# A generalized delta-rule scan in chunks: the grams of two heads as one padded 128-column product, or as two 64-row products with a bank each

## The chip, the core and the metric

The kernel runs on one core of a Trainium2 chip. The metric is the device time of one launch in microseconds: 2266.26 is the median of two runs of the kernel before, 2266.1 and 2266.43. Its engines are TensorE (PE; its weight loads are shown apart, as PEld), VectorE (DVE), ScalarE (ACT), GpSimd (POOL) and SyncE (SP, which issues the transfers).

## The reference, cut to what matters

The program is a backbone of two layers, an attention layer and a layer of RWKV-7 time mixing, each followed by an MLP. The change lies in the scan of the second layer. It runs over 256 context tokens and then 512 latent tokens, in both directions, for 16 heads of 64 features:

```
def step(s, inp):                       # s: one 64x64 state per head
    r_t, w_t, k_t, v_t, a_t, b_t = inp
    sa = jnp.einsum('bhvk,bhk->bhv', s, a_t)
    s = s * w_t[:, :, None, :] + sa[..., None] * b_t[:, :, None, :] + v_t[..., None] * k_t[:, :, None, :]
    return s, jnp.einsum('bhvk,bhk->bhv', s, r_t)
...
s_fwd, yc_fwd = wkv_scan(rc, decc[0], kc, vc, nac, bc, zero, False)      # context first
_, y_fwd = wkv_scan(r, dec[0], k, v, na, b, s_fwd, False)                # latents start from its last state
```

The kernel does not take one token at a time. It cuts the tokens into chunks of 64 and needs, for every chunk, head and direction, the masked products ("grams") of the chunk's scaled b and k vectors with its scaled a and r vectors.

## The kernel before, in words

**Groups.** The function `rwkv_scan` goes through six groups, `its[0]` to `its[5]`: a context group of four feature tiles (8 heads, 4 chunks), then two latent groups of two feature tiles each (4 heads, 8 chunks), and all this a second time for the other half of the features. A feature tile holds 128 features, that is two heads: head e=0 on partitions 0 to 63, head e=1 on 64 to 127. Every group has the scaled vectors `AR` (a and r, 64 columns each) and `BK` (b and k, 64 columns each), laid out by direction d and block (feature tile, chunk), and the grams `GM`. There are two sets of these three, used in turn: group n+2 overwrites what group n has read.

**What a group goes through.** `prep` loads the features and makes AR and BK (L1213 to L1217, after two exponentials on ScalarE, L1200 and L1201), and calls `grams` with x=0 for every feature tile and direction. `lanes` solves the triangular systems of the chunks on VectorE: a transpose (L1285) and then 30 steps of a product and a sum (L1295, L1298). `merge` brings the result back with two transposes (L1303, L1306), small matmuls (L1313, L1321) and copies into GM. `late` calls `grams` with x=1 (latent groups only, the columns of r), scales BK to the chunk's end (`to_end`, L1259) and, in `turn`, transposes BK (L1337). `chain` is the recurrence over chunks: `x_ps` (L1382, L1385), a copy `xsb`, `u_ps` (L1397), a copy into `z`, `s_ps` (L1412), and the new state `sn` on VectorE (L1423); latent groups also make the outputs `y_ps` (L1433, L1437), copied to `yt` (L1439). A chain step needs the state of the step before. `readout` normalizes and gates the outputs.

**What sets the order.** The code writes `merge` of group n+1, `prep`, `lanes` and `late` of group n+2 and so on one after the other, with `late` and the readout handed out piece by piece between the steps of the chain; a scheduler then decides, with its own estimate of each instruction, in which order every engine gets them. Each engine carries out its queue strictly in that order. The first context group's `prep` lies among the projection of v, before the scan's own memory is opened; there the grams use the PSUM tags "a" and "o". Inside the scan, all grams, the transposes of BK and the small matmuls of `merge` share a tag "g" of two banks (`gtile`).

**Grams before.** `grams(it, fl, d, x)` takes one feature tile and direction, four chunks at a time. BK of a block (128 partitions, 128 columns) is the stationary operand. AR of the two heads must not be mixed, so ScalarE copies it into one of two tiles `pad` of twice the width, head 0 into the upper half of the partitions of the left columns, head 1 into the lower half of the right columns; the other quarters were set to zero at the start (L1134). One matmul per chunk with all 128 rows then gives both heads side by side, 128 columns, and four chunks fill a bank. VectorE multiplies the bank with the mask `gmask` and writes it to GM. float32 matmuls appear in the trace as two records each.

Of the kernel before, what the change touches and what calls it, by code (L numbers as in the profile page):

```python
# [9 lines left out]
F32 = mybir.dt.float32  # L10
F32R = mybir.dt.float32r
AF = mybir.ActivationFunctionType
ALU = mybir.AluOpType
# [7 lines left out]
P = 128  # L21
# [60 lines left out]
def rconst_layout():  # L82
    names = [("gmask", 256), ("sel", 8 * 32), ("bsel", 8 * 128), ("gsel", 4 * 32), ("gbsel", 4 * 128),
             ("cen", 128), ("blk", 128)]
    off, out = 0, {}
    for n, w in names:
        out[n] = (off, w)
        off += w
    return out, off
# [56 lines left out]
LM = ()  # L146
# [24 lines left out]
class K:  # L171
# [909 lines left out]
    def rwkv_scan(self, xsave, osave):  # L1081


        nc, a, tc, ctx = self.nc, self.a, self.tc, self.ctx
# [4 lines left out]
        sa = st.enter_context(tc.tile_pool(reuse_waits=RW.get("scan_a", "pool"), name="scan_a", bufs=1))  # L1089
        rl, _ = rconst_layout()  # L1090

        def rload(name, pool, dt=F32):
            o, w = rl[name]
            t = pool.tile([P, w], dt, name=f"s_{name}")
            if dt == F32:
                nc.sync.dma_start(t, a["rconsts"][:, o:o + w])
            else:
                raw = sp.tile([P, w], F32, tag="f4", bufs=NF4, name=f"sr_{name}")
                nc.sync.dma_start(raw, a["rconsts"][:, o:o + w])
                nc.vector.tensor_copy(t, raw)  # L1100
            return t

        gmask = rload("gmask", sa).rearrange("p (d x) -> p d x", d=2)
# [10 lines left out]
        def gtile(name):  # L1114

            if pp is not None:
                return pp.tile([P, 512], F32, tag="g", bufs=2, name=name)
            gbank[0] ^= 1
            return self.ps.tile([P, 512], F32, tag="ao"[gbank[0]], name=name)
# [7 lines left out]
        lane = pa.tile([P, 32 * 32], F32, tag="lane", name="lane")  # L1127
        Lt = lane.rearrange("p (t s) -> p t s", t=32)
        MT = sa.tile([P, 32, 32], F32, tag="mt", name="mt")
        padn = [0]  # L1130
        pads = [sa.tile([P, 2, 256], F32, name=f"pad{i}") for i in range(2)]
        for t in pads:
            for e in range(2):
                nc.gpsimd.memset(t[64 - 64 * e:128 - 64 * e, e], 0.0)  # L1134

        class It:
            pass
# [15 lines left out]
        def prep(it):  # L1153
# [33 lines left out]
            def part(fl, d):  # L1187
# [28 lines left out]
                if it.lat:  # L1216
                    nc.vector.tensor_tensor(ar[:, :, 64:128], src[fl, "r"], ep[:, :, inc], ALU.mult)  # L1217
                nc.gpsimd.tensor_scalar(it.PC[:, :, fl, d], ends, 1.0, 0.0, ALU.mult, ALU.add)
                grams(it, fl, d, 0)

            return [lambda fl=fl, d=d: part(fl, d) for fl in range(it.nf) for d in range(2)]

        def grams(it, fl, d, x):


            nh, nch = it.nh, it.nch
            xs = slice(64 * x, 64 * x + 64)
            for c0 in range(0, nch, 4):
                pad = pads[padn[0] % len(pads)]
                padn[0] += 1  # L1230
                pv = pad.rearrange("p e (k x) -> p e k x", k=4)
                b = fl * nch + c0
                for e in range(2):
                    r = slice(64 * e, 64 * e + 64)
                    nc.scalar.activation(pv[r, e], it.AR[r, d, b:b + 4, xs], AF.Copy)  # L1235
                g = gtile("g_ps")
                for k in range(4):
                    nc.tensor.matmul(g[:, P * k:P * k + P], it.BK[:, d, b + k], pv[:, :, k], start=True, stop=True)  # L1238
                out = it.GM[:, d].rearrange("p (c h) x -> p c h x", h=nh)[:, c0:c0 + 4, 2 * fl:2 * fl + 2, xs]
                if x and (d, c0 // 4) in LM:  # L1240
                    nc.scalar.activation(out, g.rearrange("p (k e x) -> p k e x", k=4, e=2), AF.Copy)
                    nc.gpsimd.tensor_tensor(out, out, gmask[:, d, xs].unsqueeze(1).unsqueeze(1).to_broadcast([P, 4, 2, 64]), ALU.mult)
                    continue
                nc.vector.tensor_tensor(out, g.rearrange("p (k e x) -> p k e x", k=4, e=2),  # L1244
                                        gmask[:, d, xs].unsqueeze(1).unsqueeze(1).to_broadcast([P, 4, 2, 64]), ALU.mult)

        def late(it):

            def part(fl, d):
                if it.lat:  # L1250
                    grams(it, fl, d, 1)
                to_end(it, fl, d)

            return [lambda fl=fl, d=d: part(fl, d) for fl in range(it.nf) for d in range(2)] + [lambda: turn(it)]
# [523 lines left out]
```

## Time and profile before

| | us |
|---|---|
| median of the runs | 2266.26 |
| the profiled execution, whole | 2270.0 |
| its span from first to last instruction | 2268.2 |
| TensorE, busy | 2049.9 |
| VectorE, busy | 1320.1 |
| ScalarE, busy | 857.2 |
| ScalarE, the 160 copies into `pad` (L1235), mean of one | 0.41 |
| TensorE, the 640 records of the grams (L1238), busy | 98.1 |
| VectorE, the 80 masks (L1244), median of one | 0.684 |

All views of the profile come from the one profiled execution, and the times in them count from the start of its span. The grams are in it from 1300.3 to 1738.4 us. A row of the timeline gives start, length, engine, line, operation, output and inputs, shapes, and how many instructions are merged in it; brackets give the idle time ahead and who ended it. Lines are those of the kernel before.

### The profile page before, as it was taken

The page shows a single profiled execution, that of the slowest core. Times are in us where ns is not written, and L with a number is a line of the kernel's source. Part 1 is how long each engine was busy: PE and PEld are TensorE (multiplying, and loading weights), DVE is VectorE, ACT ScalarE, POOL GpSimd, SP SyncE. Part 2 cuts the span into 40 slices and gives each one's busy share as a digit, 9 for nine tenths or more (in the row PEclk, how much of TensorE's full clock was granted, in tenths as well). Part 3 has the DMA queues.
Part 4 walks back from the last instruction along what each step waited for, and adds up shares of the span by engine and source line. Part 5 has one row for each costly group of instructions (what it writes and reads, how often), then busy time and mean ns, then how long its engine had stood idle before and what let it go on. Part 6 is the DMA issues. An engine that isn't in the chain of part 4 may idle for free. (4 is left out here: it accounts for less than half of the span.)

```text
span 2268.2 us, 40460 instructions
## 1 busy us (share of the span) xinstructions
PE 2049.9 (90%) x16208; PEld 1668.3 (74%) x16208; DVE 1320.1 (58%) x2737; ACT 857.2 (38%) x1702; POOL 263.7 (12%) x362
## 2 busy tenths in 40 slices
PE   5989999979999999997979798698869887999999
PEld 4876756868888888885856687586658655787887
DVE  4465565464334343349787665888898657444443
ACT  4344454232111111116454445567647433222121
POOL 0122232010000000001010101000000101101110
PEclk9999999989999999997999898789889898999999
DMA  8344461122122121116146434113311312323322
GB/s 288 102 135 135 138 212 58 56 79 65 61 61 66 56 70 61 53 37 236 63 162 244 135 129 155 35 51 90 95 48 58 128 56 79 103 93 95 96 88 80
DMA packets 115885, 229.67 MB, mean 101 GB/s; under 512 B 12912, under 2 KB 31088, under 8 KB 115312
## 3 DMA queue, kind: packets, MB, share of 16 engines
q1 hardware_dynamic: 115696, 227.08, 31.1%
q8 instruction: 128, 2.10, 0.4%
q14 instruction: 61, 0.50, 0.1%
HBM read 191.80 MB, written 32.60 MB: 99 GB/s over the span
## 5 line engine op out<-in xcount | busy, mean ns | idle before, releaser
L337 DVE TENSOR_TENSOR wlo<-wraw,whi 128x1024 fp32r<-128x1024 f32 (+1 forms) x121 | 134.5, 1120 | 322.6 <-ACT whi L334 169.2
L364 PE MATMUL w_ps<-mhl,whi 128*128 128x512 f32 (+1 forms) x768 | 235.7, 361 | 7.3 <-DVE mhl L317 7.3
L362 PE MATMUL w_ps<-mhh,whi 128*128 128x512 f32 (+1 forms) x768 | 235.1, 361 | 7.1 <-POOL whi L336 3.4
L366 PE MATMUL w_ps<-mhh,wlo 128*128 128x512 f32 (+1 forms) x768 | 235.4, 361 | 5.0 <-DVE wlo L337 5.0
L364 PE MATMUL w_ps<-hid,w2h 128*128 128x512 f32 (+1 forms) x768 | 234.0, 359 | 0.0
L362 PE MATMUL w_ps<-hid,w2h 128*128 128x512 f32 (+1 forms) x768 | 231.4, 355 | 1.6 <-ACT mrelu L689 1.4
L366 PE MATMUL w_ps<-hid,w2l 128*128 128x512 f32 (+1 forms) x768 | 231.1, 355 | 0.0
L334 ACT ACTIVATE w2h<-w2raw 128x512 fp32r<-128x512 f32 x64 | 40.4, 631 | 330.0 <-PE w_ps L364 299.1
L660 DVE SCALAR_TENSOR_TENSOR X<-w_ps,ada,X 128x256 f32<-128x256 f32 (+1 forms) x128 | 73.1, 612 | 137.5 <-PE w_ps L366 137.5
L364 PEld LDWEIGHTS w_ps<-mhl,whi 128*128 128x128 f32 x768 | 127.7, 190 | 33.0 <-DVE mhl L317 9.8
L362 PEld LDWEIGHTS w_ps<-mhh,whi 128*128 128x128 f32 x768 | 127.8, 190 | 31.7 <-POOL whi L336 4.1
L366 PEld LDWEIGHTS w_ps<-mhh,wlo 128*128 128x128 f32 x768 | 127.8, 190 | 31.0 <-DVE wlo L337 8.0
L336 POOL TENSOR_SCALAR whi<-wraw 128x1024 fp32r<-128x1024 f32 (+1 forms) x60 | 69.2, 1154 | 673.2 <-PE w_ps L364 252.6
L366 PEld LDWEIGHTS w_ps<-hid,w2l 128*128 128x128 f32 x768 | 127.4, 189 | 23.3
L362 PEld LDWEIGHTS w_ps<-hid,w2h 128*128 128x128 f32 x768 | 125.5, 188 | 24.8 <-ACT mrelu L689 2.3
L334 ACT ACTIVATE whi<-wraw 128x1024 fp32r<-128x1024 f32 (+1 forms) x61 | 59.1, 968 | 222.7 <-PE w_ps L364 100.8
L364 PEld LDWEIGHTS w_ps<-hid,w2h 128*128 128x128 f32 x768 | 126.6, 188 | 20.7
L689 ACT ACTIVATE mrelu<-w_ps 128x768 f32<-128x768 f32 (+1 forms) x64 | 44.7, 699 | 189.6 <-PE w_ps L366 189.6
L1238 PE MATMUL g_ps<-pad,bk 128*128 128x128 f32 x640 | 98.1, 306 | 6.1 <-DVE gm L1244 2.1
L1238 PEld LDWEIGHTS g_ps<-pad,bk 128*128 128x128 f32 x640 | 86.0, 212 | 15.9 <-ACT pad L1235 7.5
L564 DVE CUSTOM_DVE_ANT_0 sm<-sc_ps,consts,vecs 128x256 f32<-128x256 f32 (+2 forms) x96 | 71.6, 760 | 40.7 <-PE pt_ps L585 21.9
L337 DVE TENSOR_TENSOR w2l<-w2raw,w2h 128x512 fp32r<-128x512 f32 x128 | 89.1, 697 | 4.8 <-ACT w2h L334 4.6
(381 smaller groups left out, 4486.1 us busy)
## 6 DMA issues: line engine op xcount, KB each, us to landing
ada_w<-ada_w SPq DMA_DIRECT2D x160, 256.0 KB, 3.5
wraw<-w SPq DMA_DIRECT2D x64, 512.0 KB, 3.2
w2raw<-w SPq DMA_DIRECT2D x128, 256.0 KB, 2.6
kt<-ada_w SPq DMA_DIRECT2D x32, 256.0 KB, 5.1
feat<-cs SPq DMA_DIRECT2D x16, 390.0 KB, 2.3
cs<-feat SPq DMA_DIRECT2D x24, 260.0 KB, 3.1
wraw<-wq SPq DMA_DIRECT2D x8, 512.0 KB, 3.8
wraw<-wo SPq DMA_DIRECT2D x8, 512.0 KB, 3.2
```

Of the source, the lines that this page charges most:

```text
L334: nc.scalar.activation(hi, raw, AF.Copy)
L336: nc.gpsimd.tensor_scalar(hi, raw, 1.0, 0.0, ALU.mult, ALU.add)
L337: nc.vector.tensor_tensor(lo, raw, hi.bitcast(F32), ALU.subtract)
L362: nc.tensor.matmul(o, wh, cut(xh, sl), start=start, stop=False)
L364: nc.tensor.matmul(o, wh, cut(xl, sl), start=False, stop=False)
L366: nc.tensor.matmul(o, wl, cut(xh, sl), start=False, stop=stop)
L564: nc.vector.tensor_tensor_reduce(sm[:, :nk], ps[:, :nk], self.c["band"][:, b0:b0 + nk], rs[:, h:h + 1], self.v["sink"][:, hd:hd + 1], ALU. ...
L660: self.nc.vector.scalar_tensor_tensor(self.X[:, m, sl], ps[:, sl], self.ada[:, u, m, s:s + 1], self.X[:, m, sl], ALU.mult, ALU.add)
L689: nc.scalar.activation(r, ps[:, 0:n], AF.Relu)
L1238: nc.tensor.matmul(g[:, P * k:P * k + P], it.BK[:, d, b + k], pv[:, :, k], start=True, stop=True)
```

## The change

The tiles `pad`, their memsets and ScalarE's copies go. AR is read where it stands: the two heads of a feature tile become two matmuls per chunk, one on the upper and one on the lower 64 rows of the array, each with 64 rows of BK (all 128 columns) as the stationary operand and 64 columns of AR as the moving one. Each head has a bank of its own, and a call works through all chunks of the group: 8 chunks of 64 columns fill a bank in a latent group, half of it in a context group. VectorE masks each of the two banks with one operation.

```
-            for c0 in range(0, nch, 4):
-                pad = pads[padn[0] % len(pads)]
-                ...
-                for e in range(2):
-                    r = slice(64 * e, 64 * e + 64)
-                    nc.scalar.activation(pv[r, e], it.AR[r, d, b:b + 4, xs], AF.Copy)
-                g = gtile("g_ps")
-                for k in range(4):
-                    nc.tensor.matmul(g[:, P * k:P * k + P], it.BK[:, d, b + k], pv[:, :, k], start=True, stop=True)
-                out = it.GM[:, d].rearrange("p (c h) x -> p c h x", h=nh)[:, c0:c0 + 4, 2 * fl:2 * fl + 2, xs]
-                ...
-                nc.vector.tensor_tensor(out, g.rearrange("p (k e x) -> p k e x", k=4, e=2),
-                                        gmask[:, d, xs].unsqueeze(1).unsqueeze(1).to_broadcast([P, 4, 2, 64]), ALU.mult)
+            g = [gtile("g_ps") for _ in range(2)]
+            b = fl * nch
+            for c in range(nch):
+                for e in range(2):
+                    r = slice(64 * e, 64 * e + 64)
+                    nc.tensor.matmul(g[e][:, 64 * c:64 * c + 64], it.BK[r, d, b + c], it.AR[r, d, b + c, xs],
+                                     start=True, stop=True, tile_position=(64 * e, 0))
+            out = it.GM[:, d].rearrange("p (c h) x -> p c h x", h=nh)[:, :, 2 * fl:2 * fl + 2, xs]
+            for e in range(2):
+                nc.vector.tensor_tensor(out[:, :, e], g[e][:, 0:64 * nch].rearrange("p (c x) -> p c x", x=64),
+                                        gmask[:, d, xs].unsqueeze(1).to_broadcast([P, nch, 64]), ALU.mult)
```

Behind the edited function the lines of the changed kernel have numbers that are 12 lower (L1291 for L1303, L1411 for L1423); the gram matmul is L1228 for L1238, its mask L1232 for L1244, AR and BK are 5 lower.

Since the scheduler goes by the instructions that it gets, the queues change far beyond the edited lines. The first place is VectorE's queue at the end of the lanes of `its[2]`, the second latent group, in the kernel before (`lane` and `ltmp` are the solve, `sn` the states of the chain of `its[1]`, `mt` and `dt` the merge, `bk` and `ar` the next context group):

```order
L1298 TENSOR_TENSOR lane<-lane,ltmp 128x4x9
L1423 SCALAR_TENSOR_TENSOR sn<-sn,pc,s_ps 128x128
L1298 TENSOR_TENSOR lane<-lane,ltmp 128x4x9 x2
L1295 TENSOR_TENSOR ltmp<-lane 128x30
L1295 TENSOR_TENSOR ltmp<-lane 128x27 x2
L1298 TENSOR_TENSOR lane<-lane,ltmp 128x3x10
```

That `sn` is the last one of this chain: all its updates stand ahead of the merge, whose transposes come fourteen rows later and are followed by BK and AR of the next group. In the changed kernel the same engine has, at the merge of `its[2]`:

```order
L1291 STREAM_TRANSPOSE mt<-lane 128x32x32
L1294 STREAM_TRANSPOSE dt<-lane 128x32x32
L1255 COPY gm_10960<-dt 32x32x32 x2
L1411 SCALAR_TENSOR_TENSOR sn<-sn,pc,s_ps 128x128 x2
L1232 TENSOR_TENSOR gm_10960<-g_ps,s_gmask 128x8x64 x2
L1247 TENSOR_TENSOR bk_10959<-bk_10959,pc 128x1024
L1210 TENSOR_TENSOR ar_12129<-l_kk,cs 128x4x64
```

Twenty of the 28 updates of that chain, and two of the four late calls (masks and `to_end`, L1247), have moved behind the merge; the lanes ahead hold six updates, two late calls and one long row of the solve. The same happens at the merge of `its[5]`, and at those of `its[1]` and `its[4]` with 16 of the 24 updates of the context group's chain.

The second place is TensorE's queue where late grams lie among a chain. Before, with `g_ps` in pieces of four matmuls of 128 columns:

```order
L1238 MATMUL g_ps<-pad_10964,bk_10959 128x128 x4
L1433 MATMUL y_ps<-gm_12105,z 64x64 x2
L1437 MATMUL y_ps<-ar_12103,sn 64x64 x2
L1238 MATMUL g_ps<-pad_10963,bk_10959 128x128 x4
L1385 MATMUL x_ps<-sn,ar_12103 64x128
L1382 MATMUL x_ps<-z,gm_12105 64x64 x2
L1412 MATMUL s_ps<-z,bk_12104 64x64 x4
```

And in the changed kernel, with pieces of five and nine matmuls of 64 columns:

```order
L1228 MATMUL g_ps<-ar_10958,bk_10959 128x64 x9
L1370 MATMUL x_ps<-z,gm_12131 64x64
L1400 MATMUL s_ps<-z,bk_12130 64x64
L1385 MATMUL u_ps<-xsb,gm_12131 64x64 x4
L1400 MATMUL s_ps<-z,bk_12130 64x64 x3
L1421 MATMUL y_ps<-gm_12131,z 64x64 x2
L1425 MATMUL y_ps<-ar_12129,sn 64x64 x2
L1370 MATMUL x_ps<-z,gm_12131 64x64
L1228 MATMUL g_ps<-ar_10958,bk_10959 128x64 x5
```

A call of 16 matmuls is cut where work of the chain becomes ready, so a cut may fall between the two halves of one chunk. Over the program the 320 matmuls in 62 unbroken runs become 640 in 93, of which 8 (4 before) lie in the projection of v.

More of the change, by code (lines that the diff above doesn't have):

```diff
@@ L1129, in rwkv_scan @@
         MT = sa.tile([P, 32, 32], F32, tag="mt", name="mt")
-        padn = [0]
-        pads = [sa.tile([P, 2, 256], F32, name=f"pad{i}") for i in range(2)]
-        for t in pads:
-            for e in range(2):
-                nc.gpsimd.memset(t[64 - 64 * e:128 - 64 * e, e], 0.0)
         class It:
@@ L1227, in grams @@
             xs = slice(64 * x, 64 * x + 64)
-            for c0 in range(0, nch, 4):
-                pad = pads[padn[0] % len(pads)]
-                padn[0] += 1
-                pv = pad.rearrange("p e (k x) -> p e k x", k=4)
-                b = fl * nch + c0
+            g = [gtile("g_ps") for _ in range(2)]
+            b = fl * nch
+            for c in range(nch):
                 for e in range(2):
                     r = slice(64 * e, 64 * e + 64)
-                    nc.scalar.activation(pv[r, e], it.AR[r, d, b:b + 4, xs], AF.Copy)
-                g = gtile("g_ps")
-                for k in range(4):
-                    nc.tensor.matmul(g[:, P * k:P * k + P], it.BK[:, d, b + k], pv[:, :, k], start=True, stop=True)
-                out = it.GM[:, d].rearrange("p (c h) x -> p c h x", h=nh)[:, c0:c0 + 4, 2 * fl:2 * fl + 2, xs]
[L1240 to L1244, printed above, removed]
-                                        gmask[:, d, xs].unsqueeze(1).unsqueeze(1).to_broadcast([P, 4, 2, 64]), ALU.mult)
+                    nc.tensor.matmul(g[e][:, 64 * c:64 * c + 64], it.BK[r, d, b + c], it.AR[r, d, b + c, xs],
[4 more added lines that the diff above has]
+                                        gmask[:, d, xs].unsqueeze(1).to_broadcast([P, nch, 64]), ALU.mult)
         def late(it):
```

## The prediction

> **What bounds the kernel now.** I read the page first (busy time of each engine), then the table of stretches through the scan, then VectorE's timeline, then who waits for the edited lines. In the stretches the columns are busy us (and instructions) of PE, PEld, DVE, ACT and POOL, then the granted clock.
>
> ```profile
> PE 2049.9 (90%) x16208; PEld 1668.3 (74%) x16208; DVE 1320.1 (58%) x2737; ACT 857.2 (38%) x1702; POOL 263.7 (12%) x362
> ...
> 1300.00:1325.00 25.00, 24.93 (x152) 21.34 (x150) 12.28 (x24) 9.89 (x19) 3.34 (x6) 1.00 0.44 141
> ...
> 1450.00:1475.00 25.00, 6.73 (x236) 6.50 (x238) 22.45 (x100) 7.84 (x14) 0.50 (x1) 0.50 0.11 33
> 1475.00:1500.00 25.00, 22.06 (x227) 19.98 (x223) 15.32 (x26) 17.84 (x42) 1.51 (x3) 0.77 0.30 86
> 1500.00:1525.00 25.00, 24.39 (x375) 21.08 (x374) 23.80 (x91) 17.08 (x52) 2.08 (x4) 1.00 0.07 21
> 1525.00:1550.00 25.00, 18.92 (x516) 16.25 (x518) 22.07 (x98) 16.74 (x48) 3.06 (x8) 0.90 0.21 58
> ```
>
> Over the whole program TensorE is the bound, but the page's 90% mixes stages. Ahead of the scan, where the first context group's grams lie among the v projection, PE is full (24.93 of 25). Inside the scan it is not: in 1450 to 1475 it is busy for 6.73 us while VectorE is busy for 22.45. Only in 1475 to 1500, a front, does VectorE have room (15.32).
>
> ```profile
> 1463.18 2.00 DVE L1303 STREAM_TRANSPOSE mt<-lane 128x1024 f32<-128x1024 f32 x1
> 1498.95 1.97 DVE L1285 STREAM_TRANSPOSE lane<-mt 128x1024 f32<-128x1024 f32 x1
> 1538.02 2.07 DVE L1303 STREAM_TRANSPOSE mt<-lane 128x1024 f32<-128x1024 f32 x1
> 1577.41 1.93 DVE L1285 STREAM_TRANSPOSE lane<-mt 128x1024 f32<-128x1024 f32 x1
> ...
> 1766.31 2.06 DVE L1303 STREAM_TRANSPOSE mt<-lane 128x1024 f32<-128x1024 f32 x1
> ```
>
> These transposes mark the cycle. From L1303 (merge) to L1285 (lanes) is a **front**: merge, new AR and BK, first grams; 1463.18 to 1498.95 is 35.8 us. From L1285 to the next L1303 are the **lanes**: VectorE's triangular solve, with the masks of the late grams and the chain of the group before put into its gaps; 1498.95 to 1538.02 is 39.1 us. The two alternate on VectorE until the last merge at 1766.31.
>
> ```profile
> 1520.17 0.59 DVE L1423 SCALAR_TENSOR_TENSOR sn<-sn,pc,s_ps 128x128 f32<-128x128 f32 x2
> 1524.90 0.60 DVE L1423 SCALAR_TENSOR_TENSOR sn<-sn,pc,s_ps 128x128 f32<-128x128 f32 x2
> 1528.63 0.35 DVE L1423 SCALAR_TENSOR_TENSOR sn<-sn,pc,s_ps 128x128 f32<-128x128 f32 x1
> 1533.86 0.34 DVE L1423 SCALAR_TENSOR_TENSOR sn<-sn,pc,s_ps 128x128 f32<-128x128 f32 x1
> 1540.33 0.28 ACT L1439 ACTIVATE yt<-y_ps 128x128 f32<-128x128 f32 x1 [0.78 <-PE y_ps L1437]
> ```
>
> These rows, each the first state update of a chain step, are 4.7, 3.7 and 5.2 us apart, 4.56 us on average. The chain's last copy ends at 1540.6, 2.6 us behind the merge's start: now the chain is hidden wholly beside the lanes.
>
> **The change, part by part.** The edited lines, as the trace has them:
>
> ```profile
> L1235 ACT ACTIVATE pad<-ar x160: 398/413/421, 1294.6 to 1735.5; 64x256 f32<-64x256 f32 x160
> L1238 PE MATMUL g_ps<-pad,bk x640: 272/275/583, 1300.4 to 1738.1; 128*128 128x128 f32 x160
> L1244 DVE TENSOR_TENSOR gm<-g_ps,s_gmask x80: 619/684/704, 1301.5 to 1738.4; 128x512 f32<-128x512 f32 x80
> PEld g_ps L1238: 7.5, 13
> PE g_ps L1238: 1.9, 3
> ```
>
> *ScalarE* loses 160 copies of 0.413 us, 66 us. PE and its loads waited for them 9.4 us in all (7.5 and 1.9, the last two rows), so 0 to 9.4 us is direct; the rest only lets other ScalarE work in a front start sooner. I take 2 us in the first front of a sequence and 2.5 in a context front. The four memsets of the pads on POOL go too, in the projection, where nothing waits for them.
>
> *TensorE.* 640 records of 128 columns become 1280 of 64, each with its own load of 128 columns. What a record costs:
>
> ```profile
> 68.47 1.50 PE L468 MATMUL k_ssq<-consts,k_sq 128*128 128x2 f32 x12
> ...
> 1530.42 0.34 PE L1433 MATMUL y_ps<-gm,z 128*64 128x64 f32 x4
> 1530.59 0.29 PE L1437 MATMUL y_ps<-ar,sn 128*64 128x64 f32 x4
> 1530.70 0.29 PE L1433 MATMUL y_ps<-gm,z 128*64 128x64 f32 x4
> 1530.82 0.29 PE L1437 MATMUL y_ps<-ar,sn 128*64 128x64 f32 x4
> 1530.93 0.31 PE L1397 MATMUL u_ps<-xsb,gm 128*64 128x64 f32 x2
> ...
> 1386.26 2.63 PE L1313 MATMUL mg<-mt,gm 32*32 32x32 f32 x128 [1.59 <-ACT gt L1044]
> ```
>
> Twelve matmuls of only 2 columns take 1.50 us; less the 0.25 of the last one, 11 steps of 0.114: that is the load of 128 columns, and it will bound the new form too. A latent call (16 old records) costs 16 x 0.114 = 1.82 us. The new 32 cost 3.65 if the loads of the two halves follow one another, and 1.82 if they run side by side. No row shows row halves. The nearest rows are y_ps, which alternates column halves: 16 records from 1530.42 to 1530.93, 0.032 each, though each loads and streams 64 columns, half of the 0.114. So halves of the array do work side by side there; the 32x32 quadrants of L1313 go at 2.63/128 = 0.021. I take 1.82, no change, and keep 3.65. The Trainium skill (TensorEngine Tiling (Array Packing), Key Properties) says that different tiles load and multiply in parallel; the y_ps rows agree for columns, and for rows no trace here shows it.
>
> Each time TensorE goes from such tiles to the full array and back there is a gap:
>
> ```profile
> 1503.35 0.34 PE L1433 MATMUL y_ps<-gm,z 128*64 128x64 f32 x4
> 1503.51 0.29 PE L1437 MATMUL y_ps<-ar,sn 128*64 128x64 f32 x4
> 1503.78 1.16 PE L1238 MATMUL g_ps<-pad,bk 128*128 128x128 f32 x8
> 1504.87 0.32 PE L1385 MATMUL x_ps<-sn,ar 128*64 128x128 f32 x1
> ```
>
> Eight grams occupy 1.09 us (1503.78 to 1504.87), 0.18 above 8 x 0.114; the four records before them 0.27 instead of 0.13. So 0.3 us per run of grams. The order has 93 runs for 62. The 8 in the projection, where full-array work surrounds them and PE is full, are new gaps: 8 x 0.3 = **+2.4 us**. The other runs lie in the scan, where most gaps fall on waits: of 0.3 x 27 = 8 us I count 1.
>
> *VectorE.* 80 masks of 512 elements become 64 of 512 and 32 of 256. The 256-wide one lies between 0.39 (the BK row below) and 0.684: +2.5 to +10.9 us over all, half of it ahead of the scan; in the scan I take +1, inside the rounding below.
>
> ```profile
> 1501.14 0.68 DVE L1244 TENSOR_TENSOR gm<-g_ps,s_gmask 128x512 f32<-128x512 f32 x1
> 1501.74 1.21 DVE L1259 TENSOR_TENSOR bk<-bk,pc 128x1024 f32<-128x1024 f32 x1
> 1502.87 0.26 DVE L1298 TENSOR_TENSOR lane<-lane,ltmp 128x18 f32<-128x18 f32 x2
> ...
> 1541.73 0.39 DVE L1213 TENSOR_TENSOR bk<-l_kp,en 128x256 f32<-128x256 f32 x1
> ```
>
> *The order.* This is the largest edit, and the diff does not show it. Behind the lanes' L1285 of the second latent group VectorE's queue now holds 24 of the chain's 28 updates, 8 masks, 4 to_end and a copy; in the changed order 6 updates, 4 masks and 2 to_end. Out go 18 x 0.30 + 4 x 0.60 + 2 x 1.13 + 0.6 = 10.7 us (masks and to_end by their start-to-start distances), so these lanes last 28.4. What left them stands behind the next merge, and there the chain has nothing to hide under: the merge's two transposes and copies (5.4) and five and a half steps of 4.56 (25) end it 30.5 us behind the merge's start, against 2.6 now: +28.
>
> In one sequence (context group, then two latent ones), against the times of before: ahead of the first latent group's L1285 stand 8 updates (2.4) and a mask (0.6) fewer, which with the 2 us of pads is 5 sooner. Its lanes lose 3 masks, 2 to_end, 8 updates and a copy, 7.1, so the merge at 1463.18 comes 12 sooner. The front behind it now carries 16 more context updates (4.5), 4 masks (2.4), 2 to_end (2.3) and a copy: 22 us of VectorE work become 31.5. Its old idle time of 13.5 us is kept by half, 38.5 in all (bounds 31.5 and 45): lanes at 9 sooner. The next merge: 9 + 10.7, 20 sooner. The chain's end: -20 + 28 = **8 later**. From the chain's end to the next context group's L1285 it is 36.8 us now (1540.6 to 1577.41). Of that, 2.8 of merge and 12 of the AR and BK operations (0.39 each, 4.7) come to lie ahead of the chain's end, and the pads give 2.5: 10 less, so those lanes start 2 sooner. So a sequence ends about even. The second sequence repeats it, and its chain's end, at -2 + 8 = **6 later**, is what the output projection waits for, since it reuses that group's AR, BK and GM.
>
> Sum: 6 + 2.4 + 1 = **+9.4 us**. The profiled execution lasted 2270.0 us (span 2268.2); the median of the runs is 2266.26, 3.7 less. 2270.0 + 9.4 - 3.7 = **2276 us**, no measurable change: about 2%, 45 us, can be told.
>
> *Two banks at once.* A call takes both g banks, so the next cannot begin before the second mask. In the lanes other matmuls stand between; in fronts up to 0.6 a call, 16 calls, 10 us, is in the range. Queues of DMA keep their loads; the late Z and feature loads are issued in the same sequence.
>
> **Rivals.** *Loads in turn (slower).* If the row halves' loads do not overlap, a record costs 0.114 and not 0.057. In the projection 8 context calls x 0.91 = 7.3; in latent fronts half of 16 x 1.82 (the other half waits for AR anyway) = 14.6; in the context front 3.6; late calls behind a merge 8 x 1.82 = 14.6. Together +40: 2316. It decides from a spacing of about 0.11. For it: no row shows row halves. Against: both kinds of halves that the trace shows overlap. The Trainium skill (TensorE: Matmul & The Clock Gate, LDWEIGHTS) has a load cost by its columns whatever its rows, which leaves this rival its full price; L468 shows the columns' price alone.
>
> *The chain hides again (faster).* If its steps run at the shortest gap seen, 3.7, and fronts take them in fully, a sequence saves 5.5 x 0.9 = 5 and the 8 go down to 0: two sequences, about -26: 2250. For it: VectorE is idle in fronts; against: AR and BK can't be overwritten before that chain has read them.
>
> *The chain stays out (slower, small).* If the context front gains nothing back, its 10 us stay, and steps at the longest gap seen, 5.2, add 3.5 in each sequence: +17: 2293. For it: the granted clock of 0.50 behind idle lanes (1450 to 1475).
>
> **Chances and range.** Forecast 2276 (within 2262 to 2288) 0.50; loads in turn 0.18; hides again 0.16; stays out 0.16. The range 2245 to 2318 cuts off the outer part of the first and of the second rival. Slower by over 2% (2311.6) needs the loads in turn at their full price: 0.13; faster by over 2% (2221) would take nearly all of VectorE's idle time: 0.03; within: 0.84.
>
> **What would show it.** Gram records of one call 0.057 apart, starting in pairs (0.114: the first rival). No ScalarE wait ahead of grams. L1285 to L1303 near 28 us in the two lanes of latent groups that follow a latent front; the merge at 1538 near 1518, the chain's last copy near 1549, the next L1285 within 5 us of 1577. I am wrong if the last merge isn't sooner than 1766, or if updates keep running before the merges on time.

## The result and the profile after

The changed kernel takes **2397.35 us** against 2266.26: the ratio is 1.0587, with a 95% interval of 1.0565 to 1.0609. That is 131 us slower, outside the forecast range. The profiled execution has a span of 2394.6 us against 2268.2, 126.4 more.

The page of the changed kernel, its row of engines and its row of the granted clock in 40 slices:

```profile
PE 2218.5 (93%) x16848; PEld 1829.5 (76%) x16848; DVE 1324.5 (55%) x2753; ACT 794.4 (33%) x1542; POOL 266.2 (11%) x358
...
PEclk8999999899999999989898957576666898999999
```

The same row of the kernel before:

```profile
PEclk9999999989999999997999898789889898999999
```

ScalarE lost 63 us (forecast 66), but TensorE gained 169 us of busy time, and the slices of the scan from the 24th to the 31st stand at 5 to 7 tenths of the clock where they stood at 7 to 9.

The changed kernel by stretches (busy PE, PEld, DVE, ACT, POOL, then clock):

```profile
1300.00:1325.00 25.00, 25.00 (x180) 20.91 (x179) 12.32 (x28) 7.35 (x12) 3.22 (x6) 1.00 0.41 130
...
1475.00:1500.00 25.00, 23.48 (x424) 20.92 (x426) 13.90 (x30) 12.50 (x26) 4.56 (x6) 0.70 0.08 24
1500.00:1525.00 25.00, 24.26 (x149) 22.44 (x144) 8.29 (x13) 6.07 (x12) 0.80 (x2) 0.50 0.38 117
1525.00:1550.00 25.00, 25.00 (x176) 23.62 (x175) 16.42 (x70) 5.38 (x14) 0.00 (x0) 0.50 0.00 1
```

This is new: from 1500 to 1550 TensorE is hardly ever idle and yet carries out 325 instructions, at half clock. In the same 50 us the kernel before carried out 891, though at another point of its cycle. TensorE has become the bound of this front, and VectorE (8.29 of 25) waits. The marks of the cycle in VectorE's timeline after (L1291 opens a front, L1273 the lanes):

```profile
1469.18 2.04 DVE L1291 STREAM_TRANSPOSE mt<-lane 128x1024 f32<-128x1024 f32 x1
...
1537.56 1.92 DVE L1273 STREAM_TRANSPOSE lane<-mt 128x1024 f32<-128x1024 f32 x1
...
1565.71 2.07 DVE L1291 STREAM_TRANSPOSE mt<-lane 128x1024 f32<-128x1024 f32 x1
...
1661.25 1.95 DVE L1273 STREAM_TRANSPOSE lane<-mt 128x1024 f32<-128x1024 f32 x1
...
1871.07 2.02 DVE L1291 STREAM_TRANSPOSE mt<-lane 128x1024 f32<-128x1024 f32 x1
```

The front that took 35.8 us takes 68.4 (1469.18 to 1537.56), the context front behind it 95.5 instead of 39.4. The lanes between take 28.2, as forecast. The last state update of the whole scan, after and then before:

```profile
1987.52 0.60 DVE L1411 SCALAR_TENSOR_TENSOR sn<-sn,pc,s_ps 128x128 f32<-128x128 f32 x2 [0.55 <-PE s_ps L1400]
...
1855.04 0.60 DVE L1423 SCALAR_TENSOR_TENSOR sn<-sn,pc,s_ps 128x128 f32<-128x128 f32 x2 [1.38 <-PE s_ps L1412]
```

All stages, from the starts of these marks and of that last update in each trace:

| us | before | after |
|---|---|---|
| up to the first L1285 (L1273) | 1346.1 | 1345.8 |
| five fronts, sum | 200.3 | 347.0 |
| six lanes, sum | 219.9 | 178.2 |
| last merge to the last update | 88.7 | 116.5 |
| from there to the end of the span | 413.2 | 407.1 |

So +146.7 in the fronts, -41.7 in the lanes, +27.7 from the last merge to the last update, and -6.1 behind it. Who waits in the fronts is told by the groups and by VectorE's waits (wait in us, times, longest), first after:

```profile
L1228 PE MATMUL g_ps<-ar,bk 64*128 64x64 f32 x1280 | 227.4, 384 | 22.5 <-DVE gm L1232 21.0
...
DVE gm L1232 <- PE g_ps L1228: 103.1, 37, 4.8
```

and the same wait before:

```profile
DVE gm L1244 <- PE g_ps L1238: 19.5, 17, 6.0
```

The grams occupy TensorE for 227.4 us instead of 98.1 (+129), and the masks wait 103.1 us for them instead of 19.5. One context call in the projection of v, then two pieces in a front, in TensorE's timeline after:

```profile
1303.06 1.11 PE L1228 MATMUL g_ps<-ar,bk 64*128 64x64 f32 x16
...
1501.74 6.29 PE L1228 MATMUL g_ps<-ar,bk 64*128 64x64 f32 x32
...
1509.81 3.67 PE L1228 MATMUL g_ps<-ar,bk 64*128 64x64 f32 x16 [0.74 <-DVE gm L1232]
```

In the projection a record takes 0.069 us (1.11/16), with the end of the last one in it: the halves run side by side. In the front it takes 0.20 to 0.23, three and a half to four times the forecast 0.057, and a factor of two of that is the clock.

### The profile page after: what moved, and what is told of

It reads as the page before. It is cut to its first block, busy times and chain, and to the rows that moved or that the text cites. A ratio compares the mean times of both kernels' runs of the same rounds, so it can differ in the third digit from the quotient of the medians.

```text
span 2394.6 us, 41518 instructions
## 1 busy us (share of the span) xinstructions
PE 2218.5 (93%) x16848; PEld 1829.5 (76%) x16848; DVE 1324.5 (55%) x2753; ACT 794.4 (33%) x1542; POOL 266.2 (11%) x358
## 5 line engine op out<-in xcount | busy, mean ns | idle before, releaser
L1228 PE MATMUL g_ps<-ar,bk 64*128 64x64 f32 x1280 | 227.4, 384 | 22.5 <-DVE gm L1232 21.0
L1228 PEld LDWEIGHTS g_ps<-ar,bk 64*128 64x128 f32 x1280 | 211.1, 289 | 41.6 <-DVE gm L1232 25.6
L1232 DVE TENSOR_TENSOR gm<-g_ps,s_gmask 128x512 f32<-128x512 f32 (+1 forms) x96 | 55.7, 596 | 103.2 <-PE g_ps L1228 103.1
L1370 PE MATMUL x_ps<-z,gm 128*64 128x64 f32 x768 | 87.5, 272 | 12.6 <-issue 6.4
```

Of the source, the lines that this page charges most:

```text
L1228: nc.tensor.matmul(g[e][:, 64 * c:64 * c + 64], it.BK[r, d, b + c], it.AR[r, d, b + c, xs], start=True, stop=True, tile_position=(64 * e, 0))
L1232: nc.vector.tensor_tensor(out[:, :, e], g[e][:, 0:64 * nch].rearrange("p (c x) -> p c x", x=64), gmask[:, d, xs].unsqueeze(1).to_broadcast ...
L1370: nc.tensor.matmul(x[:, 64 * e:64 * e + 64], GM[:, d, c * nh + hd, 0:64], Z[:, d, hd], start=(e == 0), stop=(first and e == 1), tile_posit ...
```

## Experiments

Ratios are to runs of the kernel before on the same chip in the same series, with 95% intervals.

**1. The matmuls by themselves.** In place of the program TensorE ran stretches of one kind of matmul, each once behind 3.5 to 5 us of idleness and once straight behind 40 wide matmuls (128x512, full array). Two of the six kinds, in short form:

```
def half(c, e): matmul(g[e][:, 64*c:64*c+64], bk[64*e:64*e+64, c], ar[64*e:64*e+64, c, 0:64], tile_position=(64*e, 0))
def alt(n):     for i in range(n): half(i // 2, i % 2)        # upper, lower, upper, ...
def runs(n):    for i in range(0, n, 16): for e in 0, 1: for c in range(8): half(c, e)
```

> Leaves out the whole backbone (the output is zeros): TensorE alone runs six kinds of matmul, each once after some us of idleness and once straight after 40 wide matmuls: 160 on the full array with 128 columns as in the kernel before; 320 on the two halves of the rows in alternation as in the kernel after; 320 on the halves in runs of eight; 320 on one half; 320 alternating with 128 columns; 320 alternating with a wide full matmul behind every eight. Theory (the row halves themselves let the granted clock fall to half, and there they cost four times as much a record): the alternating halves begin at about 0.06 us a record behind the wide matmuls, the granted clock falls to 0.50 within the stretch, and the records then take 0.19 to 0.23 us; full-array matmuls hold 0.114 and a clock near 1. Rival 1 (halves in turn at any clock): 0.11 a record from the first one on, clock 1. Rival 2 (the order of the queue or the waits on two banks cost the time, not the matmuls): 0.06 a record throughout, clock 1, about 38 us for each stretch of 320.

Stretches of that run (busy PE, PEld, DVE, POOL, then clock):

```profile
20.00:40.00 20.00, 20.00 (x180) 20.00 (x180) 0.00 (x0) 0.00 (x0) 1.00 0.00 1
160.00:180.00 20.00, 20.00 (x192) 20.00 (x190) 0.00 (x0) 0.00 (x0) 0.50 0.01 2
260.00:280.00 20.00, 19.28 (x346) 19.14 (x344) 0.69 (x1) 0.00 (x0) 1.00 0.01 2
320.00:340.00 20.00, 20.00 (x126) 20.00 (x125) 0.00 (x0) 0.00 (x0) 0.50 0.00 1
460.00:480.00 20.00, 20.00 (x126) 20.00 (x125) 0.00 (x0) 0.00 (x0) 0.50 0.00 1
580.00:600.00 20.00, 20.00 (x96) 20.00 (x95) 0.00 (x0) 0.00 (x0) 0.50 0.00 1
860.00:880.00 20.00, 20.00 (x364) 20.00 (x362) 0.00 (x0) 0.00 (x0) 1.00 0.01 2
1000.00:1020.00 20.00, 20.00 (x91) 11.44 (x91) 0.00 (x0) 0.00 (x0) 0.50 0.00 1
```

Row by row, busy time over the count: padded full array 0.111 us a record, clock 1.00 (it had this clock from its start, behind a gap of 3.49 us). Alternating halves 0.104 at clock 0.50 behind a gap, but 0.056 (19.28/346) at clock 1.00 behind the wide matmuls, for all of the stretch. Halves in runs of eight 0.16 at 0.50, both behind the gap and (460) behind the wide matmuls. One half alone 0.208 at 0.50. Alternating halves of 128 columns 0.055 at 1.00, though the stretch ahead had left the clock at half. Alternating halves with a wide matmul behind every eight: 0.50 behind a gap, and 1.00 behind the 40 wide ones. So none of the three expectations was right as a whole. Alternating halves of 64 columns don't pull the clock down; here they keep the state that they find. Halves that don't alternate do pull it down.

**2. Full height.** The slices `r` of the partitions and `tile_position` go; the order of the queues stays.

```
- nc.tensor.matmul(g[e][...], it.BK[r, d, b + c], it.AR[r, d, b + c, xs], ..., tile_position=(64 * e, 0))
+ nc.tensor.matmul(g[e][...], it.BK[:, d, b + c], it.AR[:, d, b + c, xs], ...)
```

> The kernel after with one thing changed: each gram matmul takes all 128 rows instead of one half of them (64 columns, two banks, as many matmuls, the same order of every queue). The grams then mix the two heads, so the values are not the reference's. Theory (row halves hold the clock down): the granted clock in the scan is back near that of the kernel before, a latent call of 32 records takes 1.9 to 3.7 us instead of 6.3, and the time falls from 2397 to between 2270 and 2330. Rival (changed order of chain and merge, or the two banks at once): within 15 us of 2397.

2396.26 us, ratio 1.0582 (1.0551 to 1.0612): the time of the changed kernel. One call in the projection, one piece in a front:

```profile
1300.20 1.89 PE L1228 MATMUL g_ps<-ar,bk 128*128 128x64 f32 x16
...
1422.38 3.68 PE L1228 MATMUL g_ps<-ar,bk 128*128 128x64 f32 x16
```

My theory fell here: with all 128 rows, where nothing can overlap, a record in the front costs what it cost with halves. So in the fronts the halves had not overlapped. The clock is 0.50 from 1410 to 1440 here too, so the low clock does not belong to row halves alone.

**3. The two loops exchanged** (`for e` outside, `for c` inside).

> The kernel after with the two loops of a gram call exchanged: first all matmuls of the upper half, then all of the lower. If halves of unlike rows overlap when they alternate, the overlap is lost: 0.11 a record in the value projection and more than 0.23 in the scan at half clock, so 2400 to 2520 in all. If they go one after the other anyway, the time stays within 20 us of 2397.

2397.0 us in one run: nothing changed, as expected for the case that they go one after the other anyway. Only the projection shows the loss of the overlap (1.60 us a call for 1.11). This led back to the order, this time with the numbers of the buffers, which the rows in the part on the change lack. TensorE's queue in a latent front of the changed kernel:

```
L1228 MATMUL g_ps_12356<-ar1_12129,bk1_12130 128x64 x8
L1400 MATMUL y_ps_12142<-z_12151,bk0_10959 64x64 x3
L1228 MATMUL g_ps_12357<-ar1_12129,bk1_12130 128x64 x8
L1400 MATMUL y_ps_12142<-z_12151,bk0_10959 64x64 x3
L1228 MATMUL g_ps_12394<-ar1_12129,bk1_12130 128x64 x8
```

Eight matmuls of one head, a piece of the chain, then eight of the other. The code alternates; the queue of the fronts doesn't. In the projection the scheduler left the pairs together, and in the late calls it did so in part. Why it parts them was not tested; my reading is that the two banks come free one after the other, and that it hands out all that is ready for the bank that is free.

**4. Alternation enforced.**

```
+ m = nc.tensor.matmul(...)
+ if c or e:
+     tc.keep_in_program_order(m)
```

> The kernel after, with every gram matmul of a call but the first tied in the queue behind the one traced before it, so that upper and lower half really alternate in the scan; the results are the same. New theory (in the scan the queue holds eight matmuls of one half and then eight of the other, so nothing overlaps and 32 records take 6.6 us at half clock): the latent call falls to 1.8 to 3.4 us, the granted clock in the scan rises above 0.75, and the time falls from 2397 to between 2255 and 2310. Rival 1 (the changed order of chain and merges costs the time): still over 2370. Rival 2 (64-column halves hold the clock at half even when they alternate, at 0.104 us a record as in the cold stretch of the run of single stretches): 2310 to 2350.

2344.23 us, ratio 1.0341 (1.0306 to 1.0377). Of the 5.9% the lost alternation was 2.5, some 56 us (the fronts fall from 347.0 to 301.1); the time lies in the second rival's range, and the record is near its 0.104. A whole latent call now, still at half clock:

```profile
1421.24 3.68 PE L1228 MATMUL g_ps<-ar,bk 64*128 64x64 f32 x32
```

0.115 a record, as in the stretch behind a gap.

**5. More columns streamed.** The 64 columns of AR twice (`unsqueeze(1).to_broadcast([64, 2, 64])`), chunks from the last to the first, the halves not tied.

> The kernel after with the same loads, as many records and the halves still one after the other, but each matmul streams its 64 columns twice (128 columns, the second copy overwritten by the next chunk); the results are the same. If the low clock is what doubles the cost (loads of 128 columns behind only 64 streamed columns leave the clock at half), 128 streamed columns keep it near full: 0.11 us a record, a latent call near 3.6 us, and 2300 to 2350. If the clock stays at half because of the halves as such, 0.21 us a record and 2390 to 2420. If only the order of the queue counts, 2390 to 2400.

2381.73 us, ratio 1.0516 (1.0492 to 1.0541): in none of the three ranges, some 16 us less than the changed kernel, which I can't explain. The record stays at 3.67/16 us, so in halves that don't alternate 128 streamed columns don't bring the clock back:

```profile
1420.61 3.67 PE L1229 MATMUL g_ps<-ar,bk 64*128 64x128 f32 x16
```

**6. The clock.** Ahead of each latent front's first call, in the pinned kernel:

```
+ w = gtile("warm_ps")
+ for c in range(8):
+     nc.tensor.matmul(w, it.BK[:, d, b + c], it.BK[:, d, b:b + 4].rearrange("p c x -> p (c x)"), ...)
```

> The pinned kernel with eight extra full-array matmuls of 512 columns (their result is not used) ahead of the first gram call of each latent front; all other results are unchanged. If the low clock is what is left of the loss (in the run of single stretches alternating halves kept a clock of 1.00 for 35 us behind wide matmuls, and 0.50 for as long behind idleness), the fronts' records fall from 0.115 to about 0.06 us: each of four fronts of four calls of 32 records loses 7 us, and later work at full clock some 5 to 10 us more, against 7 to 13 us for the extra matmuls: 2300 to 2350 in all, with the granted clock in the fronts from 0.50 to over 0.75. If the clock falls back whatever ran ahead of the halves: clock 0.50 again and 2365 to 2395.

2334.85 us, ratio 1.0305 (1.0273 to 1.0338). The same call as in experiment 4:

```profile
1404.24 8.62 PE L1227 MATMUL warm_ps<-bk 128*128 128x512 f32 x15
...
1414.05 2.00 PE L1232 MATMUL g_ps<-ar,bk 64*128 64x64 f32 x30
1416.82 2.39 PE L1232 MATMUL g_ps<-ar,bk 64*128 64x64 f32 x32
```

0.067 to 0.075 a record where it was 0.115: with the clock up, the halves cost about what I had forecast. The 8.7 to 9.6 us that the wide matmuls take in each of the four latent fronts eat most of it: the intervals of pinned and pinned_warm overlap.

**7. Halves in some places only.** Condition in `grams`: halves (pinned, but for the first of these) where it holds, padded grams with copies elsewhere. `fl` is 0 for a group's first feature tile, and `x` is 1 in the late calls.

| label | halves for | us | ratio (95%) |
|---|---|---|---|
| first_only | `it.n == 0`, not pinned | 2261.8 | 0.9981 (0.9964 to 0.9999) |
| mixed | `fl or x` | 2317.53 | 1.0226 (1.0196 to 1.0256) |
| front_halves | `fl and not x` | 2263.37 | 0.9997 (0.9981 to 1.0014) |
| late_halves | `x` | 2282.46 | 1.0081 (1.0057 to 1.0106) |

> Row halves only for the first context group, whose grams stand between the value projection's matmuls; the other groups keep padded columns and copies as before. Theory: the clock is held up there by the projection, the halves go at 0.06 a record, and the time is that of the kernel before, 2258 to 2276. Rival (halves in turn, or a drain at each change between halves and full array, about 0.06 to 0.3 us apiece): 128 matmuls in that group add 5 to 15 us, 2272 to 2281.

> Padded full-array grams with copies, as before, for the first feature tile of each front; pinned alternating halves for the second tile and for the late calls; results unchanged. If full-array grams bring the clock up and alternating halves then hold it, most of the copies are saved at full clock: 2245 to 2270. If halves let the clock fall wherever they stand: 2290 to 2340.

> Pinned halves for the second feature tile in the fronts alone, padded grams with copies for the first tile and in all late calls; results unchanged, queues nearly as in the kernel before. If the late halves are what is left: 2250 to 2268, with the lanes at 35 us or more and the tail below 90. If it is the fronts: 2285 to 2315.

> Padded grams with copies in every front, pinned alternating halves in the late calls alone; results unchanged. The queues then differ in the two halves of the scan: chain and late calls are spread as in mixed up to the third front, and nearly as in the kernel before from the fourth on. If the late halves between the chain's steps are what is left: 2290 to 2315. If it is the fronts: 2255 to 2275.

In the projection halves cost nothing on balance. In the fronts they cost nothing either, if padded full-array grams come first and they alternate; in front_halves (first tile padded, the others in halves) a call is, once more, at full clock:

```profile
1414.94 2.40 PE L1234 MATMUL g_ps<-ar,bk 64*128 64x64 f32 x32
```

What is left, 2.3% from front_halves to mixed, some 52 us, comes with halves in the late calls. With them alone, in late_halves, it is 0.8%, some 18 us, in neither of the ranges expected. This run shows both costs: in the first sequence of groups its third lanes are nearly bare of the chain (6 updates) and take 28.2 us, as in mixed, and in the second its sixth lanes hold the chain (23 updates) and take 37.8, nearly as before (24 updates, 39.7). A piece of a late call in each:

```profile
1445.19 3.67 PE L1234 MATMUL g_ps<-ar,bk 64*128 64x64 f32 x30 [0.25 <-DVE gm L1240]
...
1755.66 0.88 PE L1234 MATMUL g_ps<-ar,bk 64*128 64x64 f32 x10
```

and its stretches there:

```profile
1425.00:1450.00 25.00, 16.29 (x180) 14.79 (x180) 25.00 (x125) 2.00 (x6) 1.04 (x2) 0.62 0.04 12
...
1750.00:1775.00 25.00, 24.32 (x421) 21.28 (x418) 25.00 (x111) 13.23 (x43) 1.04 (x2) 1.00 0.07 18
```

From the first merge to the fourth L1285 it loses 19 us against the kernel before (224.2 for 204.9), from there to the chain's end nothing (277.2 for 277.6), with the same late halves. So the late halves cost time in the sequence whose lanes stand bare (there VectorE is full, TensorE has 16 us of work in 25, the clock is at 0.62), and none in the other.

**8. The order of chain and merge.** First a priority for the chain (`HP = 1000`), then a tie of each merge behind the chain ahead of it (`with tc.issue_after(its[n - 2].last): merge(its[n - 1])`).

| label | kernel | us | ratio (95%) |
|---|---|---|---|
| pinned_hp | pinned, priority | 2348.66 | 1.0374 (1.0356 to 1.0391) |
| mixed_hp | mixed, priority | 2301.58 | 1.0153 (1.0132 to 1.0174) |
| before_hp | before, priority | 2265.53 | 1.0004 (0.9991 to 1.0017) |
| after_ord | after, tie | 2400.74 | 1.0593 (1.0574 to 1.0612) |
| mixed_ord | mixed, tie | 2311.21 | 1.0202 (1.0181 to 1.0222) |

> The pinned kernel with a higher priority for the chain's instructions, so that on VectorE 10 fewer updates of the last chain but one stand behind the merges (28 instead of 36 after the last merge, as in the kernel before); results unchanged. If what is left of the loss is the order: 2344 falls by 20 to 60 us. If it is the clock of the halves: within 10 us of 2344.

> The mixed kernel (padded grams for the first feature tile, pinned halves for the second and for late calls) with the same priority for the chain; 28 updates instead of 40 behind the last merge. Order: 2317 falls to 2260 to 2295, the tail of 116 us behind the last merge to about 90. Clock of the halves: within 10 us of 2317.

> The kernel before with the same priority, the control: its chain already stands ahead of the merges, so 2255 to 2275; a time far below would say that the priority is worth something by itself.

> The kernel after with each merge of a scan group queued behind the last update of the chain ahead of it, as it stands in the kernel before; results unchanged. If updates behind the merge are what the order costs: the third front falls from 95 to about 50 us, the tail keeps 28 updates, the lanes grow by the chain's time, and the whole is 2340 to 2375. If the place of the merge is of no account (the chain takes its time on either side of it): 2385 to 2410, what the front loses comes back ahead of the merge.

> The same tie in the mixed kernel (padded grams for the first feature tile, pinned halves for the rest). Order costs: 2317 falls to 2265 to 2295. Place of the merge of no account: 2305 to 2330, the third front shorter by what the lanes ahead of it grow.

The place of the merge is of no account. In mixed_ord the third front falls from 84.8 to 48.9 us, and the lanes ahead of it grow from 28.2 to 59.3; after_ord shows the same (95.5 to 65.6, 28.2 to 61.9). Priority helped mixed by 16 us, to a time between its two ranges: 34 less behind the last merge (116.1 to 81.9), of which half comes back in the fronts and lanes. It helped pinned not at all, so the order is no cause that works by itself.

Nor are bare lanes. The sixth lanes of mixed_ord and of late_halves both hold the chain and the late halves: 24 and 23 updates, and 8 masks and 4 `to_end` in each (mixed_ord first, columns as in the other stretches):

```profile
1756.77:1811.66 54.89, 46.63 (x658) 40.71 (x656) 38.82 (x174) 19.80 (x66) 3.52 (x7) 0.78 0.06 16
...
1741.06:1778.84 37.78, 36.12 (x632) 31.54 (x630) 37.57 (x171) 18.66 (x63) 3.11 (x6) 1.00 0.07 19
```

Nearly the same work takes 54.9 us at a mean clock of 0.78 and 37.8 at 1.00. In these two, the late halves cost time where the clock falls and none where it holds. What lets it fall in the one and not in the other stays open: no run changed that alone.

**9. What the copies are worth.** First the copies left out (zeros for the pads); then the second of each pair on GpSimd; then three pads for two.

```
- nc.scalar.activation(pv[r, e], it.AR[r, d, b:b + 4, xs], AF.Copy)
+ if e: nc.gpsimd.tensor_copy(pv[r, e], it.AR[r, d, b:b + 4, xs])
+ else: nc.scalar.activation(pv[r, e], it.AR[r, d, b:b + 4, xs], AF.Copy)
```

> The kernel before without ScalarE's 160 copies: the padded columns are constant zeros, so the grams are zeros (the computation of the grams is left out, not its matmuls). It shows what the copies alone are worth. By the prediction's term (2 us in the projection's fronts and 2.5 us in the late calls): 2255 to 2266. If the copies stand on the path in every front (0.83 us times 80 calls): 2200 to 2210.

> The kernel before with the second of each pair of pad copies on GpSimd instead of ScalarE; results unchanged. If the 22 us that the copies cost are the 0.83 us for which the pair holds up each front's first grams, two engines side by side give back up to half: 2253 to 2262. If GpSimd takes more than 0.83 us for a copy or delays VectorE, 2262 to 2290.

> The kernel before with three pad buffers instead of two; results unchanged. If the copies cost time because they wait for a pad to come free of its matmuls, 2250 to 2260; if by their own length, 2262 to 2268.

no_copies takes 2243.76 us, ratio 0.9916 (0.9888 to 0.9944): 13 to 25 us faster, between the two ranges expected. pool_split takes 2254.06, **0.9955 (0.9942 to 0.9967)**: about half of that comes back, and this version beats both kernels. pads3 takes 2263.66, 0.9994 (0.9982 to 1.0006): no wait for a free pad. GpSimd's copies are slower than ScalarE's 0.413, but stand beside them:

```profile
L1236 POOL COPY pad<-ar 64x256 f32<-64x256 f32 x80 | 42.0, 530 | 132.7 <-PE g_ps L1241 66.5 <-DVE ar L1215 57.0 <-issue 4.8
```

## Why the prediction was wrong, step by step

- **TensorE, "I take 1.82, no change": the step that failed.** Its premise, that halves of the rows load side by side, is right: 0.056 a record alone, 0.067 to 0.069 with the last one's end. But I took the alternation from the code, not from the queue, where eight of one half stand ahead of eight of the other; the rows of the order that I read had the buffers' numbers left out. The alternation is worth 56 us.
- **The same step's clock.** I priced a record at the rate of full clock and let the granted clock appear in one rival only. Halves that don't alternate hold it at 0.50, even behind wide matmuls, so 32 records cost 6.3 to 7.3 us instead of 1.82 or 3.65. The step from pinned to mixed, 26 us, I put down mostly to this, and the step from mixed to front_halves, 52 us, to the late calls where the clock falls. With the 56 us the three steps lead back to the time of the kernel before. That the clock is what the 26 and the 52 us go by is argued from the records and the lanes above; no run changed it alone (pinned_warm raised it in the fronts, at the cost of its wide matmuls).
- **The rival "loads in turn"** named the right side, at 2316, and its fronts and late calls did lose. Its reason was wrong (the order of the queue parts the halves, not the array), so was its term for the projection (7.3 us, where nothing was lost), and its price lacked the factor of the clock.
- **ScalarE.** "0 to 9.4 us is direct" was read from PE's waits alone; leaving the copies out is worth 13 to 25 us, and the fronts shrink from 200.3 to 182.9 in all. That a front's first grams follow AR by the copies' length fits this, and pool_split's gain. So the change had more to win than I gave it: if the two add up, about 19 won by the copies and 150 lost by the rest make its 131.
- **The order.** The lanes came as forecast (28.4; measured 28.2 and 28.1), and that the place of the merge is of no account was right, as after_ord and mixed_ord show. That a sequence ends about even was wrong. The merge expected at 1518 came at 1565.7, 48 us later: some 30 of them because the front ahead of it, forecast at 38.5 with bounds of 31.5 and 45, took 68.4, and 18 because the first latent front, which I had expected to end 5 sooner, grew from 55.3 to 69.8. The bounds held VectorE's work and left out TensorE's. The chain did come out behind the merges, but I sized it too low: I had it end 30.5 us behind them, and its last update starts 45.0 and 38.5 us behind the merges at 1565.71 and 1871.07. The last merge, which had to come sooner than 1766, came at 1871, the sign that I had named for being wrong.
- **VectorE** (+4.4 us busy) and the **gaps in the projection** (+2.4 forecast; first_only, which has them, lost nothing on balance) were small, as forecast. No run took the two banks at once by themselves; front_halves, whose calls in halves take both, lost nothing.

## What to carry to other kernels

Matmuls that are to share the array must stand next to each other in the queue, not only in the code: look for it with buffer numbers, and tie them together where the queue parts them. Price small matmuls at both clocks, and ask what holds the clock up in that stage, since a TensorE that is busy all the time can still run at half. What a copy ahead of a matmul costs is what the stage saves without it, not only the wait that the matmul shows.

## What the runs showed of the hardware

TensorE at 100% busy stayed at a granted clock of 0.50 for over 60 us (halves in runs, 300 to 380; one half, 540 to 660). The Trainium skill (TensorE: Matmul & The Clock Gate, Part 1: The HAM clock gate) says that a busy window of about 3.4 us brings the clock to full; these stretches, of 80 and 120 us, differ, and they decide: it depends on what keeps TensorE busy. Alternating halves of 64 columns had two lasting states, 0.104 us a record at 0.50 (69 us long) and 0.056 at 1.00 (36 us), by what ran ahead; of 128 columns they rose to 1.00 by themselves. What quantity the clock follows is not settled by these runs: 128 streamed columns in halves that don't alternate (3.67 us for 16 records), and 64 columns at full height (3.68), both ran in the fronts at 0.50.
